# Issuing the experts' loop of a decoder trunk in a written order on every engine

## The chip, the cores and the metric

The kernel runs on one core of one Trainium2 chip. The metric is the device time of one execution in microseconds, lower is better. Before the change the median of three runs is 1376.91 us (1375.65 to 1377.59).

## The reference, cut to what matters

A trunk of two layers over 256 tokens of width 1024, float32 throughout. The change touches only the last block, the top-2-of-8 experts:

```python
logits = xt @ w_router                       # 256 x 8
top_logits, top_idx = lax.top_k(logits, 2);  gates = softmax(top_logits)
for e in range(8):                           # as blocks of gathered tokens
    y_e = (silu(x_e @ w_gate[e]) * (x_e @ w_up[e])) @ w_down[e]   # 1024 -> 3584 -> 1024
y[token] += gate * y_e[slot];  x = x + g2 * y;  out = rmsnorm(x) * final_gain
```

All eight experts are computed, so 8 x 3 x 1024 x 3584 float32 weights (336 MiB) are read once each.

## The kernel before

Layer 0, the pooling mixer and the router come first (to about 450 us). Then the experts' loop runs to the end.

**Blocks.** An expert's hidden width of 3584 is cut in seven blocks of 512 (`NJ`). A block is three weight tiles of 128 x 4096 float32: gate, up and down. The expert in place 0 has seven narrow blocks, done first. After that three wide places (1 to 3, up to 128 tokens) and four narrow places (4 to 7, up to 64 tokens) alternate in groups of seven blocks, in the order wide, narrow, wide, narrow, wide, narrow, narrow (`BLOCKS`, line 55). The down tile of a block is used two blocks after its gate and up tiles. Which expert stands at a place is found on the chip from the counts (`ordering`) and read into a register of SP before that expert's first load.

**Halves.** Each tile arrives as two halves of 128 x 2048 (1 MiB, `load`, line 126) in a ring of buffers: six of tag `raw`, four of `e8`, two that stay (`cb`, `T_l`), and `qk`, `a8`, `kd` for some loads at the start (`SPARE`, line 59). Each half is split into an upper and a lower part (`split`, line 112): ScalarE copies it rounded to `w_hi`, VectorE subtracts to `w_lo`. There are three pairs of `w_hi` and `w_lo` buffers (`N_SPL`), so a half can be split once TensorE has done with the half three before it. `raw` is free when `w_lo` is written.

**Matmuls.** A wide half takes 12 matmuls of 512 columns (`mm3`: hi times hi, hi times lo, lo times hi), a narrow one 8 (`mm2`: both parts of 64 tokens stand side by side in one 128-column stationary operand, and `fold_T` adds them with 16 small matmuls against `fold`).

**Around the matmuls.** `take_out` or `silu` empties a gate's or up's PSUM bank on ScalarE. `moe_T` (wide) or `fold_T` (narrow) turns the hidden block and splits it to `dT`. `prepare` gathers a place's tokens with 16 matmuls per half (`gather`, with its split in the same step). `combine` scales an expert's output by `g2_row` to `y_g`, splits it to `yp` and scatters it to `xs` with four `give` steps. Such steps wait in two lists and one is run after each tile.

**Order.** The program is traced in the order of the source, but the order in which each engine issues is chosen by a planner that takes what its own cost model thinks is ready first. `behind(...)` adds edges: the evacuation of a tile's PSUM bank and the turn of the previous block are queued behind the split of the last half of the next tile (`behind_next`, line 835).

Of the kernel before, what the change touches and what calls it, by code (L numbers as in the profile page):

```python
# [19 lines left out]
P = 128  # L20
# [44 lines left out]
def trunk(ctx, tc, x, cols, c_row, const, ada_0, ada, w_0, w_in, w_out, f_gu, f_dn, pool_w, m_g, m_u, m_d, out):  # L65
# [57 lines left out]

    ring = deque([("raw", N_RAW, ALWAYS)] * N_RAW)

# [10 lines left out]
    def weights(src, step=2048, held=((), (), (), ()), in_halves=False):  # L136

        parts, splits = [], []
        for h in range(0, src.shape[1], 2048):
            t = load(src[:, h:h + 2048], in_halves)  # L140
            hi = buf("w_hi", [2048], N_SPL, R)
            lo = buf("w_lo", [2048], N_SPL, R)
# [452 lines left out]
    n_blocks = NE * NJ  # L595
    expert = [0] + [None] * (NE - 1)

    def sources():

        def rows(a, i):  # L600
            p, j = BLOCKS[i]
            if p == 0:
                return a[j * P:(j + 1) * P, :]
            if expert[p] is None:
                expert[p] = nc.values_load(place_i[0:1, p - 1:p], engines=[SP], min_val=1, max_val=NE - 1,
                                           skip_runtime_bounds_check_because="a permutation of 1 to 7")
            return a[ds((expert[p] * NJ + j) * P, P), :]

        for i in range(n_blocks + 2):
            if i < n_blocks:  # L610
                yield rows(m_g, i)
                yield rows(m_u, i)
            if i > 1:
                yield rows(m_d, i - 2)

    srcs = sources()


    once = [ring[i][:2] + (1,) for i in range(2)]
# [32 lines left out]
    def ordering():  # L652
# [5 lines left out]
        cnt = small([NE], "cnt")  # L658
        nc.vector.tensor_copy(cnt, ps[:, 0:NE])
# [9 lines left out]
        nc.vector.tensor_reduce(rank, over.rearrange("p e i j -> p e (i j)"), axis=AX.X, op=ALU.add)  # L669
        at = tmp[:, 2 * N * N:3 * N * N].rearrange("p (r e) -> p r e", r=N)  # L670
# [11 lines left out]
        nc.vector.tensor_copy(place_i, place)  # L682
        placed = []
        for name, a in (("slot", slot), ("sel", sel), ("gate", gate)):
# [3 lines left out]
            placed.append(t)  # L688

# [11 lines left out]
        return place_i, placed, room, most_i  # L701
# [13 lines left out]
    def prepare(xe, slots, sels, narrow=False):  # L715


        oh = None
        ohT = buf("ohT", [T], N_OHT, R)
        ns = HALF if narrow else P  # L720

        def gather(n):
            nonlocal oh
            if n == 0:
                oh = one_hot(slots, sels, narrow)
            ps = tbank()[:, 0:4 * ns]
# [4 lines left out]
            ps = ps.rearrange("p (c t) -> p c t", c=4)  # L731
# [6 lines left out]
        def back():  # L738
            ps = tbank()
            for b in range(TB):  # L740
                nc.tensor.transpose(ps[:, tok(b)], oh[:, b], ident)
            nc.scalar.activation(ohT, ps[:, 0:T], AF.Copy)

        return xe, ohT, [lambda n=n: gather(n) for n in range(2)] + [back]
# [16 lines left out]
    def hidden(pg, pu):  # L761
        sg = w2([512], "sg")
        nc.scalar.activation(sg, pg, AF.Silu)
        hd = w2([512], "moe_h")
# [3 lines left out]
    def moe_T(hd):  # L768
        ps = transpose4(hd)
        th = buf("dT", [2, 4, P], 2, R, name="dT")  # L770
        split(th[:, 0], th[:, 1], ps.rearrange("p (c t) -> p c t", c=4))
        return th
# [6 lines left out]
    def fold_T(gu):  # L779
# [8 lines left out]
        nc.vector.tensor_mul(hd, ps[:, 1], sg)  # L788
        th = buf("dT", [4, 2, HALF], 2, R, name="dT")
        split(th[:, :, 0], th[:, :, 1], hd)  # L790
        return th
# [10 lines left out]
    def combine(ye, ohT, gates, g2_row, last=False):  # L802

        yp = buf("kd", [1 if last else 2, D], dt=F if last else R, name="yp")

        def take(n):
            c = slice(512 * n, 512 * (n + 1))
            t = yp[:, 0, c] if last else w2([512], "y_g")
            nc.vector.tensor_mul(t, ye[n], g2_row[:, c])
            if not last:  # L810
                split(yp[:, 0, c], yp[:, 1, c], t)

        def give(n, b):
            c = slice(512 * n, 512 * (n + 1))
            ps = tbank()
            if last:
                nc.tensor.matmul(ps, ohT[:, tok(b)].bitcast(F), yp[:, 0, c], start=True, stop=True)
            else:
                nc.tensor.matmul(ps, ohT[:, tok(b)], yp[:, 0, c], start=True, stop=False)
                nc.tensor.matmul(ps, ohT[:, tok(b)], yp[:, 1, c], start=False, stop=True)  # L820
            nc.vector.scalar_tensor_tensor(xs[:, b, c], ps, gates[b], xs[:, b, c], op0=ALU.mult, op1=ALU.add)

        return [lambda: (take(0), take(1))] + [lambda n=n, b=b: give(n, b) for n in range(2) for b in range(TB)]
# [8 lines left out]
    with behind(root, chosen):  # L832
        coming = weights(next(srcs), 1024)

    def behind_next():

        return behind(*coming.splits[len(coming.splits) // 2]) if coming else nullcontext()

    def advance():
        nonlocal coming  # L840
        at, src = coming, next(srcs, None)
        coming = None if src is None else weights(src)
        return at

    steps, first_steps = [], []

    def step():
        if first_steps or steps:
# [187 lines left out]
```

## Time and profile before

| what | value |
|---|---|
| median of 3 runs | 1376.91 us |
| the profiled execution | 1374.36 us, of which the span of its instructions is 1372.6 us |
| PE busy | 1316.0 us (96%) |
| DVE busy | 1217.4 us (89%) |
| ACT busy | 966.0 us (70%) |
| DMA | 477.30 MB, mean 348 GB/s |
| mean granted TensorE clock | 0.991 |

PE is TensorE, DVE is VectorE, ACT is ScalarE, SP issues all loads. Busy shares are averages over stages. Matmuls overlap each other in the pipeline, so a busy PE is not PE at its peak. Times below are from the start of the span. The experts' loop is cut into stretches at the start of a DVE split: 458.9 (half 2), 556.3 (half 38, the first of the alternating blocks), and then every 42 halves, that is every seven blocks, to 1340.8 (half 332 of 336).

### The profile page before, as it was taken

What the parts mean: (1) busy time and instruction counts of PE and PEld (TensorE: products, weight loads), DVE (VectorE), ACT (ScalarE), POOL (GpSimd) and SP (SyncE); (2) the same over time, 40 slices, a digit from 0 to 9 for tenths busy, and PEclk for the clock granted to TensorE, in tenths of its full rate; (3) what the DMA queues carried; (4) which work ended last, traced back from release to release, by engine and by line L of the source; (5) the groups of instructions that cost most, each with busy time, mean ns of one, the idle gap of its engine ahead of it and who ended that gap; (6) DMA issues with size and microseconds to landing.
All of it is one profiled execution on the core that took longest, in us unless ns stands there. A gap on an engine that the chain in (4) does not pass through costs nothing.

```text
span 1372.6 us, 16765 instructions
## 1 busy us (share of the span) xinstructions
PE 1316.0 (96%) x6146; PEld 1054.7 (77%) x6146; DVE 1217.4 (89%) x1119; ACT 966.0 (70%) x889; POOL 0.2 (0%) x4
## 2 busy tenths in 40 slices
PE   7999998999999999999999999999999999999996
PEld 5687877888887768778778877788778777777874
DVE  6889876998766799999989999989999989999997
ACT  6655465444435698878878877878877868788884
POOL 0000000000000000000000000000000000000000
PEclk9999999999999899999999999999999999999998
DMA  9976886899746999999999999999999999999960
GB/s 381 366 277 251 330 297 222 306 391 375 307 164 257 359 384 373 368 379 413 420 374 397 424 349 340 406 363 426 411 362 408 366 350 394 401 362 416 424 284 33
DMA packets 66474, 477.30 MB, mean 348 GB/s; under 512 B 7377, under 2 KB 7761, under 8 KB 8658
## 3 DMA queue, kind: packets, MB, share of 16 engines
q1 hardware_dynamic: 66386, 476.17, 88.6%
q8 instruction: 50, 0.82, 0.2%
q14 instruction: 38, 0.31, 0.1%
HBM read 475.10 MB, written 1.05 MB: 347 GB/s over the span
## 4 chain that ended last, share of the span: by engine, by line
PE 70%; DVE 15%; DMA 6%; ACT 4%; issue 4%; SPq 0%; DVEq 0%; ACTq 0%
PE bank L157 15%; PE bank L158 15%; PE bank L156 15%; DVE w_lo L113 11%; PE bank L749 8%; PE bank L748 7%; PE tbank L784 4%; DMA raw<-in_m_d_dram 3%; ACT w_hi L113 2%; DMA raw<-in_m_u_dram 2%; PE tbank L730 2%; PE tbank L256 1%; DVE raw L167 1%; DMA raw<-in_m_g_dram 1%; DMA col<-in_cols_dram 1%
## 5 line engine op out<-in xcount | busy, mean ns | idle before, releaser
L113 DVE TENSOR_TENSOR w_lo<-raw,w_hi 128x2048 fp32r<-128x2048 f32 (+1 forms) x413 | 907.8, 2225 | 91.2 <-ACT w_hi L113 87.3
L113 ACT ACTIVATE w_hi<-raw 128x2048 fp32r<-128x2048 f32 (+1 forms) x413 | 763.0, 1865 | 196.1 <-PE bank L158 147.4
L749 PE MATMUL bank<-w_lo,xe_n 128*128 128x512 f32 x560 | 230.9, 413 | 14.4 <-DVE w_lo L113 11.4
L748 PE MATMUL bank<-w_hi,xe_n 128*128 128x512 f32 x560 | 220.8, 395 | 0.0
L749 PEld LDWEIGHTS bank<-w_lo,xe_n 128*128 128x128 f32 x560 | 105.6, 189 | 59.9 <-DVE w_lo L113 40.5
L156 PE MATMUL bank<-w_hi,T_h 128*128 128x512 f32 x352 | 140.9, 401 | 3.1 <-ACT T_h L113 3.1
L157 PE MATMUL bank<-w_lo,T_h 128*128 128x512 f32 x352 | 139.2, 395 | 2.4 <-DVE w_lo L113 2.4
L158 PE MATMUL bank<-w_hi,T_l 128*128 128x512 f32 x352 | 139.2, 396 | 0.6 <-DVE T_l L113 0.5
L157 PE MATMUL bank<-w_lo,xe 128*128 128x512 f32 x336 | 132.8, 395 | 0.7 <-DVE w_lo L113 0.6
L156 PE MATMUL bank<-w_hi,xe 128*128 128x512 f32 x336 | 131.5, 391 | 0.0
L158 PE MATMUL bank<-w_hi,xe 128*128 128x512 f32 x336 | 131.0, 390 | 0.0
L748 PEld LDWEIGHTS bank<-w_hi,xe_n 128*128 128x128 f32 x560 | 105.8, 189 | 18.8 <-ACT w_hi L113 0.2
L167 DVE SCALAR_TENSOR_TENSOR raw<-raw,cb 128x1024 f32<-128x1024 f32 x96 | 114.4, 1218 | 0.0
L749 PE MATMUL bank<-w_lo,dT 128*128 128x512 f32 x280 | 104.5, 411 | 6.4 <-DVE w_lo L113 5.8
L157 PE MATMUL bank<-w_lo,dT 128*128 128x512 f32 x256 | 100.9, 394 | 0.9 <-DVE w_lo L113 0.8
L748 PE MATMUL bank<-w_hi,dT 128*128 128x512 f32 x280 | 99.8, 393 | 1.7 <-DVE dT L113 1.7
L158 PE MATMUL bank<-w_hi,dT 128*128 128x512 f32 x256 | 99.9, 390 | 0.0
L156 PE MATMUL bank<-w_hi,dT 128*128 128x512 f32 x256 | 93.5, 389 | 0.0
L156 PEld LDWEIGHTS bank<-w_hi,T_h 128*128 128x128 f32 x352 | 66.8, 190 | 17.6 <-ACT T_h L113 3.7
L157 PEld LDWEIGHTS bank<-w_lo,T_h 128*128 128x128 f32 x352 | 66.8, 190 | 16.6 <-DVE w_lo L113 2.8
L158 PEld LDWEIGHTS bank<-w_hi,T_l 128*128 128x128 f32 x352 | 66.9, 190 | 15.5 <-DVE T_l L113 1.5
L157 PEld LDWEIGHTS bank<-w_lo,xe 128*128 128x128 f32 x336 | 63.1, 188 | 17.1 <-DVE w_lo L113 4.7
(231 smaller groups left out, 1417.9 us busy)
## 6 DMA issues: line engine op xcount, KB each, us to landing
raw<-in_m_g_dram SPq DMA_DIRECT2D x112, 1024.0 KB, 7.1
raw<-in_m_u_dram SPq DMA_DIRECT2D x112, 1024.0 KB, 7.2
raw<-in_m_d_dram SPq DMA_DIRECT2D x112, 1024.0 KB, 7.2
raw<-in_ada_dram SPq DMA_DIRECT2D x48, 1024.0 KB, 7.1
raw<-in_f_gu_dram SPq DMA_DIRECT2D x22, 1024.0 KB, 6.5
raw<-in_w_in_dram SPq DMA_DIRECT2D x16, 1024.0 KB, 4.9
raw<-in_f_dn_dram SPq DMA_DIRECT2D x11, 1024.0 KB, 6.9
raw<-in_w_dram SPq DMA_DIRECT2D x8, 1024.0 KB, 7.7
```

What stands on the lines that cost most here:

```text
L113: return nc.scalar.activation(hi, src, AF.Copy), nc.vector.tensor_sub(lo, src, hi.bitcast(F))
L156: nc.tensor.matmul(ps, xh, wh, start=start, stop=False)
L157: nc.tensor.matmul(ps, xh, wl, start=False, stop=False)
L158: nc.tensor.matmul(ps, xl, wh, start=False, stop=stop)
L167: nc.vector.scalar_tensor_tensor(s, s, 1.0, cb, op0=ALU.mult, op1=ALU.mult, accum_out=mod[:, m:m + 1])
L256: nc.tensor.transpose(ps[:, i * P:(i + 1) * P], src[:, i * P:(i + 1) * P], ident)
L730: nc.tensor.matmul(ps[:, i * ns:(i + 1) * ns], xm[:, b, c], oh[:, b, 0:ns], start=(b == 0), stop=(b == TB - 1))
L748: nc.tensor.matmul(ps, x, wh, start=start, stop=False)
L749: nc.tensor.matmul(ps, x, wl, start=False, stop=stop)
L784: nc.tensor.matmul(ps[:, i, c], a[:, c * P:(c + 1) * P], fold, start=True, stop=True)
```

## The change

The loop is put in a region in which each engine issues in the order of the source (`tc.manual_schedule()`); the planner's choice and the `behind` edges are gone there. `PROGRAM` lists the 168 tiles: gate and up of block i, then down of block i-2. Each tile's turn emits, in this order: its matmuls; load and split of one half, four halves ahead; its evacuation; the turn of the previous block (the narrow one's split to `dT` one tile later); one step; load and split of a second half. A fourth pair of split buffers is made of `cb` and `T_l`, which leave the load ring, as does `qk` (now `y_g`). `gather` and its split, `back` and its copy, `give` and its add become steps of their own, and so do the parts of `ordering`; a step that leaves a PSUM bank full is followed by its partner. `f_row` and the load of the square-root table move to the end of the loop. Two matmuls of `ident` and `xs` ahead of the loop, whose result nothing reads, are dropped.

```diff
-SPARE = ((8, "a8", 2, 2), (11, "kd", 1, 3), (12, "qk", 1, 10), (12, "cb", 1, ALWAYS), (9, "T_l", 1, ALWAYS))
+SPARE = ((8, "a8", 2, 2), (11, "kd", 1, 3))
+PROGRAM = [("d", BLOCKS[i - 2]) if what == "d" else (what, BLOCKS[i]) for i in range(NE * NJ + 2) for what in "gud"
+           if (i > 1 if what == "d" else i < NE * NJ)]
+AHEAD = 4
+    halves = deque([("w_hi", "w_lo", N_SPL)] * N_SPL)
...
+    halves.append(("cb", "T_l", 1))
-    ps = tbank()
-    for _ in range(2):
-        nc.tensor.matmul(ps, ident, xs[:, 1, 0:512], start=True, stop=True)
+    def fetch(step=2048):
+        src = next(feed, None)
+        if src is not None:
+            t, (hi, lo) = load(src), halves_of()
+            for c in range(0, 2048, step):
+                split(hi[:, c:c + step], lo[:, c:c + step], t[:, c:c + step])
+            stream.append((hi, lo))
...
-        return xe, ohT, [lambda n=n: gather(n) for n in range(2)] + [back]
+        return xe, ohT, [hot, lambda: gather(0), lambda: parts(0), lambda: gather(1), lambda: parts(1) or back(), back_out]
...
-        return [lambda: (take(0), take(1))] + [lambda n=n, b=b: give(n, b) for n in range(2) for b in range(TB)]
+        def scaled():
+            to = y_g
...
+            for n in range(2):
+                nc.vector.tensor_mul(to[:, half(n)], ye[n], g2_row[:, half(n)])
+
+        def upper():
+            st["yp"] = buf("kd", [2, D], dt=R, name="yp")
+            for n in range(2):
+                nc.scalar.activation(st["yp"][:, 0, half(n)], y_g[:, half(n)], AF.Copy)
+
+        def lower():
+            yp = st["yp"]
+            for n in range(2):
+                nc.vector.tensor_sub(yp[:, 1, half(n)], y_g[:, half(n)], yp[:, 0, half(n)].bitcast(F))
...
+        steps = [scaled] if last else [scaled, upper, lower]
+        for n in range(2):
+            for b in range(TB):
+                steps += [lambda n=n, b=b: give(n, b), lambda n=n, b=b: add(n, b)]
+        return steps
...
+    def step():
+        nonlocal held
+        queue = held or first_steps or steps
+        if queue:
+            held = queue if queue.pop(0)() else None
...
+    with tc.manual_schedule():
+        while len(stream) < AHEAD:
+            fetch()
+        for n, (what, block) in enumerate(PROGRAM):
+            p, j = block
+            wide = WIDE[p]
+            if what == "d":
+                if j == 0:
+                    outs[p] = [bank(), bank()]
+                if block == BLOCKS[-1]:
+                    turn(block)
+                    while block not in ths:
+                        turn()
+                down(next_weights(), ths.pop(block), outs[p], j == 0, j == NJ - 1, not wide)
+                fetch()
+                if j == NJ - 1:
+                    while p == NE - 1 and (first_steps or steps):
+                        step()
+                    finish_combine(p)
+                    if p < NE - 1:
+                        steps.pop(-11)()
+            else:
+                if what == "g":
+                    while held or first_steps and first_steps[0] in ready[p][2]:
+                        step()
+                ps = up(next_weights(), ready[p][0], not wide)
+                fetch()
+                i = BLOCKS.index(block)
+                if what == "g":
+                    gates[block] = silu(ps) if wide else take_out(ps, "g_out")
+                    if i:
+                        turn(BLOCKS[i - 1])
+                else:
+                    sg = gates.pop(block)
+                    mid[block] = hidden(sg, ps) if wide else (sg, take_out(ps, "u_out"))
+                    turn()
+                    if block == (0, 0):
+                        gate, g2_row = gating()
+                        steps.extend([lambda it=ordering(known): next(it, None)] * 8)
...
+            step()
+            fetch()
+        f_row = row(y_gs[:, 1], col[:, C_FG:C_FG + KD])
+        table(AF.Sqrt, xs[:, 0, 0:1])
+        while steps:
+            step()
```

## Rows read from the trace of the kernel before

**Rows 1.** The view by windows: busy us (instructions) of PE, PEld, DVE, ACT, POOL; clock, DMA.

```profile
458.90:556.30 97.40, 92.50 (x482) 75.19 (x481) 90.92 (x91) 85.27 (x76) 0.00 (x0) 0.99 0.98 379
556.30:664.90 108.60, 106.59 (x488) 84.29 (x487) 104.99 (x66) 89.60 (x66) 0.00 (x0) 1.00 0.98 390
664.90:775.00 110.10, 108.91 (x519) 87.65 (x518) 101.72 (x62) 89.67 (x67) 0.00 (x0) 1.00 0.99 400
775.00:891.60 116.60, 112.49 (x530) 90.27 (x529) 112.28 (x79) 92.36 (x71) 0.00 (x0) 1.00 0.96 372
891.60:1006.50 114.90, 111.72 (x532) 89.41 (x531) 106.17 (x67) 91.20 (x70) 0.00 (x0) 1.00 0.98 394
1006.50:1124.60 118.10, 114.66 (x566) 93.45 (x565) 108.54 (x73) 92.41 (x73) 0.00 (x0) 1.00 0.97 376
1124.60:1235.80 111.20, 107.98 (x501) 85.77 (x501) 105.16 (x66) 89.61 (x68) 0.00 (x0) 1.00 0.98 384
1235.80:1340.80 105.00, 104.14 (x477) 82.94 (x476) 100.25 (x58) 88.87 (x64) 0.00 (x0) 1.00 0.88 366
```

**Rows 2.** Waits of DVE and of ACT, 556.3 to 1340.8: total, times, longest us.

```profile
DVE w_lo L113 <- ACT w_hi L113: 35.2, 55, 1.7
...
ACT w_hi L113 <- PE bank L158: 62.9, 79, 2.0
...
ACT xe_n L113 <- PE tbank L730: 12.4, 6, 3.8
```

**Rows 3.** The timeline of DVE and of ACT: splits back to back (start, us, count).

```profile
646.55 13.30 DVE L113 TENSOR_TENSOR w_lo<-raw,w_hi 128x2048 fp32r<-128x2048 f32 x6
...
1250.57 5.53 ACT L113 ACTIVATE w_hi<-raw 128x2048 fp32r<-128x2048 f32 x3 [0.32 <-ACT sg L763]
```

**Rows 4.** The chain of waits: start, us, what stood in it.

```profile
523.18 1.78 PE tbank L730 x16
...
531.09 1.73 PE tbank L784 x16
...
1187.47 0.50 PE bank L157
1187.97 0.23 PE bank L158
```

**Rows 5.** The timeline of the loop's start.

```profile
446.20 3.43 PE L627 MATMUL tbank<-xs,kp 128*128 128x512 f32 x4
...
458.90 2.28 DVE L113 TENSOR_TENSOR w_lo<-raw,w_hi 128x2048 fp32r<-128x2048 f32 x1
...
462.96 13.44 DVE L113 TENSOR_TENSOR w_lo<-raw,w_hi 128x2048 fp32r<-128x2048 f32 x6 [1.78 <-ACT w_hi L113]
```

**Rows 6.** The view by windows, five microseconds at the loop's start (columns as in Rows 1).

```profile
455.00:460.00 5.00, 5.00 (x21) 4.66 (x21) 1.86 (x3) 1.15 (x3) 0.00 (x0) 0.50 1.01 418
```

**Rows 7.** The timeline of the loop's end.

```profile
1338.59 4.49 DVE L113 TENSOR_TENSOR w_lo<-raw,w_hi 128x2048 fp32r<-128x2048 f32 x2
...
1343.80 1.31 ACT L113 ACTIVATE yp<-y_g 128x512 fp32r<-128x512 f32 x2 [0.85 <-DVE y_g L809]
...
1349.63 0.41 DVE L788 TENSOR_TENSOR h_n<-tbank,sg_n 128x256 f32<-128x256 f32 x1
...
1350.52 1.28 ACT L232 ACT_TABLE_LOAD   x1
1351.81 0.20 ACT L232 ACTIVATE tab<-xs 128x1 f32<-128x1 f32 x1
...
1352.63 0.50 PE L748 MATMUL bank<-w_hi,dT 128*128 128x512 f32 x1 [1.67 <-DVE dT L113]
...
1357.08 1.28 DVE L809 TENSOR_TENSOR yp<-bank,g_row 128x512 f32<-128x512 f32 x2
...
1359.05 1.54 DVE L821 SCALAR_TENSOR_TENSOR xs<-tbank,gate_p,xs 128x512 f32<-128x512 f32 x2 [0.69 <-PE tbank L817]
```

**Rows 8.** DMA issues by line: KB each, median us to landing.

```profile
raw<-in_m_g_dram SPq DMA_DIRECT2D x112, 1024.0 KB, 7.1
```

More of the change, by code (lines that the diff above doesn't have):

```diff
@@ L759, in up, with silu, hidden @@
         return ps
-    def hidden(pg, pu):
+    def silu(pg):
         sg = w2([512], "sg")
         nc.scalar.activation(sg, pg, AF.Silu)
+        return sg
+    def hidden(sg, pu):
         hd = w2([512], "moe_h")
@@ L800, in down, with combine @@
                     mm3(ye[n], th[:, 0, c], th[:, 1, c], wh, wl, first and c == 0, last and c == 3)
[L802 to L811, printed above, removed]
+    def combine(ye, ohT, gates, g2_row, y_g, last=False):
+        st = {}
+        half = lambda n: slice(512 * n, 512 * (n + 1))
+        def scaled():
+            to = y_g
+            if last:
+                st["yp"] = buf("kd", [1, D], name="yp")
+                to = st["yp"][:, 0]
+            for n in range(2):
[8 more added lines that the diff above has]
+                nc.vector.tensor_sub(yp[:, 1, half(n)], y_g[:, half(n)], yp[:, 0, half(n)].bitcast(F))
@@ L821, in give, with add @@
-            nc.vector.scalar_tensor_tensor(xs[:, b, c], ps, gates[b], xs[:, b, c], op0=ALU.mult, op1=ALU.add)
-        return [lambda: (take(0), take(1))] + [lambda n=n, b=b: give(n, b) for n in range(2) for b in range(TB)]
+                for i in range(2):
+                    nc.tensor.matmul(ps, ohT[:, tok(b)], yp[:, i, half(n)], start=(i == 0), stop=(i == 1))
+            return True
+        def add(n, b):
+            c = half(n)
+            nc.vector.scalar_tensor_tensor(xs[:, b, c], st.pop("ps"), gates[b], xs[:, b, c], op0=ALU.mult, op1=ALU.add)
@@ L832, in trunk @@
     with behind(root, chosen):
[L833 to L843, printed above, removed]
+        for _ in range(2):
+            fetch(1024)
     steps, first_steps = [], []
+    held = None
     def step():
-        if first_steps or steps:
-            (first_steps or steps).pop(0)()
@@ L851, in turned_of @@
[L851 to L852 removed]
+        nonlocal held
+        queue = held or first_steps or steps
+        if queue:
+            held = queue if queue.pop(0)() else None
     def picked(a, placed, p):
         return pick(a, 0) if p == 0 else pick(placed, p - 1)
[L857 to L868 removed]
+    y_gs = buf("qk", [2, D], name="y_g")
@@ L870, in prepare_next, with finish_combine @@
+    gates, mid, ths, outs, known = {}, {}, {}, {}, []
+    turning = None
+    def finish_combine(p):
+        steps.extend(combine(outs[p], ready[p][1], picked(gate, known[1][2], p), g2_row, y_gs[:, len(outs) % 2], p == NE - 1))
     def prepare_next(p):
+        slot_p, sel_p, _ = known[1]
         ready[p] = prepare(xe_of(p), pick(slot_p, p - 1), pick(sel_p, p - 1), not WIDE[p])
         first_steps.extend(ready[p][2])
[L876 to L904 removed]
@@ L905, in trunk, with turn @@
-    ths[n_blocks - 1] = turned_of(n_blocks - 1, mid)
-    down_of(n_blocks - 2)
-    while steps:
-        step()
-    last = coming
-    down_of(n_blocks - 1)
-    steps += combine(outs[NE - 1], ready[NE - 1][1], picked(gate, gate_p, NE - 1), g2_row, True)
-    with behind(last.splits[-1][0]):
-        table(AF.Sqrt, xs[:, 0, 0:1])
-    while steps:
-        step()
+    def turn(block=None):
+        nonlocal turning
+        if block is not None:
+            turning = block, (moe_T if WIDE[block[0]] else fold_T)(mid.pop(block))
+        if turning is not None:
+            th = next(turning[1])
+            if th is not None:
+                ths[turning[0]] = th
+                turning = None
@@ L917, in finish @@
+    place_i, _, room, most_i = known
     def finish():
@@ L947, in trunk @@
                 at = ds((e * NJ + j) * P, P)
-                hd = hidden(up(weights(m_g[at, :]), xe), up(weights(m_u[at, :]), xe))
-                down(weights(m_d[at, :]), moe_T(hd), ye, j == 0, j == NJ - 1)
-            for step in combine(ye, ohT, [ge[:, b] for b in range(TB)], g2_row):
+                hd = hidden(silu(up(weights(m_g[at, :]), xe)), up(weights(m_u[at, :]), xe))
+                down(weights(m_d[at, :]), next(moe_T(hd)), ye, j == 0, j == NJ - 1)
+            for step in combine(ye, ohT, [ge[:, b] for b in range(TB)], g2_row, y_gs[:, 0]):
                 step()
```

124 lines of the change are left out of this document (50 added, 74 removed).

## The prediction

> **What bounds the kernel now.** I read the view by windows first, cut where DVE begins a given split. In the seven stretches of seven blocks [rows 1] DVE is busy 739.1 of 784.5 us, and PE shows 99% in the fastest of them. So two engines are near full at once, and the idle 45.4 us of DVE in these seven, with 6.5 us in the stretch ahead of them, bound what a better order alone can win: 52 us. The waits say what the idle time is: DVE waits 35.2 us for the upper part of the next half, and ACT waits 62.9 us for TensorE to give back a split buffer [rows 2]. A half costs DVE 2.21 us back to back (13.30 for six, the last one 0.08 longer) and ACT 1.85 us (5.53 for three) [rows 3]. A matmul costs 0.23 us, the first one after a wait 0.50, 16 folds 1.73, 16 gathers 1.78 [rows 4]. Seven blocks are then 42 x 2.21 + 6.7 for turning the blocks (four narrow, two instructions of 0.41 each [rows 7]; three wide, two of twice that size) = 99.5 us of DVE, and 408 x 0.23 + 4 x 1.73 + 1.3 = 102 us of PE. The last stretch, which has neither a combine nor a gather, takes 105.0, with DVE idle for 4.75 of it [rows 1].
>
> What the steps add I fit to the same rows. The first stretch has one combine: 108.6 - 105.0 = 3.6 us. The second has one gather: 5.1 us. The sixth has a combine and `f_row`, so `f_row` is 2.6. All seven hold 6 combines and 5 gathers: 7 x 105.0 + 6 x 3.6 + 5 x 5.1 + 2.6 = 784.7, against 784.5 measured.
>
> **The change part by part. Start of the loop.** With three pairs the split of half 3 waits for TensorE's first half; DVE idles 1.78 us and starts it at 462.96 [rows 5]. With four it follows half 2, and half 4 starts near 463.0 instead of 465.2: -2 us.
>
> The two dropped matmuls are 3.43 us on PE ahead of the ranking matmuls [rows 5]; in their place PE mostly waits for DVE, so I count 0. The bounds are -1 and +2.5: in 455 to 460 the granted clock is 0.50, the lower level, though they ran 6 us earlier [rows 6], and another 5 us at that level would cost half of it. The Trainium skill ("TensorE: Matmul & The Clock Gate", What's actually happening) holds that the low clock is the default and activity releases it, which speaks against dropping them; by it the sum would be up to 2.5 us higher.
>
> **First stretch.** Past that 1.78 us, 4.7 us of DVE idle are left. I walked narrow blocks through the written order (each instruction at the later of its engine's turn and its input): DVE never waits, since ACT ends the later half's upper part 1.1 us before DVE wants it. One wait comes with `gating`, now one piece: Exp and its table load (1.28 us, as in rows 7) and two row copies sit ahead of the next upper part, about 3 us of idle DVE. So -1.7.
>
> **The seven stretches, without steps.** The fourth pair gives ACT one more half of lead, but the written order spends it. The split of a tile's second new half stands behind the evacuation and, after a narrow block, behind the folds (1.73 us after the gate's last matmul) and their Silu. Walking one group of 21 tiles: after the three fold turns ahead of a wide gate DVE idles 1.6, 0.8 and 0.8 us, at two wide downs 0.5 each, and 0.65 in small pieces: 4.85 of idle on 99.5 of work, 104.4 us per group against 105.0. That is -0.6 x 7 = -4. Bounds: -3 per group (two thirds of the idle gone) to +2.5 per group (half as much idle again).
>
> **Combines.** `scaled` (DVE) and `upper` (ACT) fall in the same tile, and the next upper part of a weight half is queued behind `upper`. DVE's next split waits for 1.31 of `upper` [rows 7] and 1.92 of the upper part: 3.2 us idle. Some of that replaces idle the group has anyway; the walk with a combine gives +5.6 against 3.6 measured, so +2.0 for places 0, 5, 2 and 6. For places 4 and 1 gather steps come in between, and the cost stays: together +8.
>
> **Gathers.** ACT's 12.4 us of waits for gather matmuls [rows 2] go, because the split comes one tile later. I take 3.0 us (PE 3.6 and DVE 1.5 per gather, each half hidden) for 5.1: -2.1 x 3. For wide places 2 and 3 the last gathered part stands behind a weight split on DVE, and PE waits some 2.3 us for it: +0.2 x 2. Together -6. `f_row` leaves this stage: -2.6.
>
> **End.** Place 3's combine comes with the third last tile, and nothing hides it. From the start of the split of half 332: splits and turn 2.2 + 0.35 + 2.2 + 2.2 = 6.95, `scaled` 1.28, `upper` 1.31, upper part 1.92, last split 2.28, `lower` 1.28, then the turn of the last block, which the order puts behind the down before it (0.41 + 0.42 + 0.42), and 16 matmuls, 3.95: 20.2 us. Now it is 1357.08 - 1340.8 = 16.3 [rows 7]: +3.9. After it, four adds of place 3 run, which were hidden (0.65 + 4 x 0.72 = 3.5), the second transposes and copy of `f_row` (0.45 + 0.65), the table load (1.28) and its one-column read of `xs` (0.20), which the next add must wait for: 6.2 us to the last expert's first add, against 1.97 now [rows 7]: +4.2. So +8.1, with bounds +4 and +10. The profile shows the table load at 1.28 us with the next activation 0.01 behind [rows 7]. The Trainium skill ("ScalarE: Activation LUTs", What ACT_TABLE_LOAD costs) adds a drain of about 1.38 us to each; by that the end would be 1.4 us later, and the trace does not agree.
>
> **Loads** cost nothing. A ring of ten halves covers 10 x 2.5 = 25 us against 7.1 from issue to landing [rows 8]. SP's order and register reads are the same.
>
> **Sum.** -2 - 1.7 - 4 + 8 - 6 - 2.6 + 8.1 = -0.2. The profiled execution took 1374.36 us (1.76 around the span), 2.55 under the median; the same difference on the median of 1376.91 gives 1376.7, so 1377.
>
> **The rivals.** *Given back in part only* (faster): the fourth pair absorbs the waits my walk leaves, so DVE's idle falls to 3 us per group (-12 for -4), and the combine's bubble falls where PE is the late one (+2 for +8). The sum is -14, about 1362. For it: ACT's 62.9 us of buffer waits is what one more pair attacks. Against: PE itself is 99% busy in the plain stretch.
>
> *Slower, by one mechanism*: ACT's lead of 1.1 us in front of the later half. Each of 56 blocks passes through evacuation and turn in order; a wait of 0.2 us per handoff is in my walk. If handoffs and interleaved steps eat more than those 1.1 us, each further 0.1 us stalls DVE in every block, 5.6 us. At 0.3 beyond, +17: 1394. For it: the planner could put a ready split ahead of a late evacuation, a fixed order can't. Against: PE and DVE alternate as the late one, which hides some.
>
> *The order is nearly what the planner had* (evacuations were already queued behind splits), and the end overlaps more than I think: 1376.
>
> **Chances.** Balance, as forecast (1370 to 1384 by itself): 0.44. Faster rival: 0.29. Slower rival: 0.20. Same order: 0.07. A measurement tells about 0.2%, 2.75 us, from no change. From balance 0.10 falls below that band, 0.19 in it and 0.15 above. So faster 0.39, same 0.26, slower 0.35. The range reaches into both rivals: 1355 to 1392.
>
> **What would show it.** After: DVE idle 30 to 45 us in the seven stretches; a gap of some 3 us on DVE behind the scaling of places 0, 5, 2 and 6, with ACT's split behind `yp`; no waits of ACT for gather matmuls; the last expert's first add 22 to 26 us after the split of half 332 begins, against 18 now. A loop with DVE idle under 25 us, or an end no longer than now, makes the prediction wrong on the fast side; ACT's splits regularly ending after DVE is free, on the slow side.

## The result, and the profile after

The changed kernel takes 1383.36 us (median of 5 runs, 1383.0 to 1390.71) against 1375.69 us before, run beside it (median of 5 runs, 1372.58 to 1377.59): ratio 1.0068, 95% interval 1.0039 to 1.0096. So it is slower by 0.7%, 5 to 13 us. The profiled execution has a span of 1381.0 us against 1372.6, a mean granted clock of 0.982 against 0.991.

The stretches after, cut at the same halves as [rows 1] (half 2, half 38, then every 42 halves; the last row is from half 332 to the end). The columns are those of [rows 1].

```profile
460.16:558.70 98.54, 89.51 (x448) 73.32 (x447) 91.45 (x89) 81.72 (x71) 0.00 (x0) 0.96 0.95 359
558.70:669.62 110.92, 107.95 (x511) 87.33 (x510) 104.78 (x67) 88.74 (x70) 0.00 (x0) 1.00 0.98 383
669.62:777.58 107.96, 106.52 (x519) 88.16 (x518) 100.95 (x61) 88.20 (x68) 0.00 (x0) 1.00 1.00 411
777.58:892.67 115.09, 109.74 (x533) 90.86 (x532) 109.34 (x74) 91.93 (x72) 0.00 (x0) 1.00 0.98 386
892.67:1004.70 112.03, 109.65 (x525) 90.18 (x524) 105.29 (x68) 90.09 (x70) 0.00 (x0) 0.98 0.99 403
1004.70:1120.93 116.23, 109.75 (x550) 91.61 (x549) 107.69 (x72) 89.22 (x68) 0.00 (x0) 1.00 0.98 377
1120.93:1234.96 114.03, 108.06 (x505) 87.97 (x504) 107.08 (x68) 90.17 (x69) 0.00 (x0) 1.00 0.98 382
1234.96:1340.03 105.07, 104.22 (x493) 85.61 (x491) 100.48 (x58) 88.69 (x67) 0.00 (x0) 1.00 0.93 384
1340.03:1381.00 40.97, 23.41 (x89) 16.24 (x87) 22.68 (x30) 12.78 (x21) 0.00 (x0) 0.80 0.08 28
```

The seven stretches take 781.3 us (784.5 before): some are shorter (second, third, fourth, fifth), those of places 0 and 6 are longer (first, sixth), and the plain one is what it was. The loop's start up to half 38 ends 2.4 us later (558.70 against 556.3), and the end is 9.2 us longer (41.0 against 1372.6 - 1340.8 = 31.8). 2.4 - 3.2 + 9.2 = +8.4, the difference of the spans.

What stands in the waits of the seven stretches (558.7 to 1340; total us, times, longest us), against [rows 2]:

```profile
DVE w_lo L118 <- ACT w_hi L118: 42.8, 52, 2.5
...
ACT w_hi L118 <- PE bank L168: 55.4, 63, 2.4
ACT sg_n L820 <- PE tbank L818: 27.6, 25, 1.1
ACT w_hi L118 <- PE bank L778: 20.7, 17, 3.2
ACT yp L853 <- DVE y_g L848: 16.4, 4, 5.3
...
ACT xe_n L118 <- PE tbank L753: 1.7, 2, 0.9
...
PE tbank L867 <- DVE xs L872: 10.7, 7, 2.9
```

The waits for gather matmuls went (12.4 to 1.7), as the change meant. But ScalarE now waits 16.4 us in four pieces for `y_g` (7.1 us in six before), and VectorE's waits for the upper part grew from 35.2 to 42.8. The last line is new: TensorE's scatter matmuls (`give`) wait 10.7 us for VectorE's add to `xs`, which empties a PSUM bank and stands behind a weight split on VectorE's queue. Before, no wait of TensorE for that add is among its waits in these stretches. Neither kernel is held up by its loads here: in the seven stretches ScalarE waits 8.1 us for loads before, and neither it nor VectorE waits for one after. The timeline of place 0's combine shows the first two at once:

```profile
597.62 1.28 DVE L848 TENSOR_TENSOR y_g<-bank,g_row 128x512 f32<-128x512 f32 x2
601.40 4.49 DVE L118 TENSOR_TENSOR w_lo<-raw,w_hi 128x2048 fp32r<-128x2048 f32 x2 [2.50 <-ACT w_hi L118]
...
598.33 1.23 ACT L853 ACTIVATE yp<-y_g 128x512 fp32r<-128x512 f32 x2 [5.28 <-DVE y_g L848]
599.47 3.71 ACT L118 ACTIVATE w_hi<-raw 128x2048 fp32r<-128x2048 f32 x2
```

ScalarE had nothing to wait for but `y_g`: it stood 5.28 us with `yp` at the head of its queue, ran it, and only then began the next half's upper part, for which VectorE then stood 2.50 us. The same 2.50 us stands behind the scaling at 992.8, 1093.2, 1192.8 and 1347.0 (places 5, 2, 6 and 3), and behind those of places 4 and 1 it doesn't.

The end, from the same timeline (compare [rows 7]):

```profile
1346.97 1.28 DVE L848 TENSOR_TENSOR y_g<-bank,g_row 128x512 f32<-128x512 f32 x2
1350.75 2.29 DVE L118 TENSOR_TENSOR w_lo<-raw,w_hi 128x2048 fp32r<-128x2048 f32 x1 [2.50 <-ACT w_hi L118]
...
1355.54 0.80 PE L778 MATMUL bank<-w_hi,dT 128*128 128x512 f32 x1 [6.37 <-DVE dT L118]
1356.13 0.63 PE L779 MATMUL bank<-w_lo,dT 128*128 128x512 f32 x1
...
1365.79 1.25 ACT L203 ACTIVATE y_g<-tbank 128x512 f32<-128x512 f32 x2 [10.76 <-PE tbank L197]
1367.06 1.28 ACT L242 ACT_TABLE_LOAD   x1
1368.36 0.20 ACT L242 ACTIVATE tab<-xs 128x1 f32<-128x1 f32 x1
1368.59 1.41 DVE L872 SCALAR_TENSOR_TENSOR xs<-tbank,gate_p,xs 128x512 f32<-128x512 f32 x2 [1.69 <-ACT tab L242]
```

The last expert's first add comes 28.6 us after the split of half 332 begins (1368.59 - 1340.03; 18.3 before). The copies of `f_row`, the table load and its one-column read stand one behind the other ahead of it.

### The profile page after: what moved, and what is told of

Its sections match the earlier page's. It is cut to its first block, busy times and chain, and to the rows that moved or that the text cites. A ratio compares the mean times of both kernels' runs of the same rounds, so it can differ in the third digit from the quotient of the medians.

```text
span 1381.0 us, 16731 instructions
## 1 busy us (share of the span) xinstructions
PE 1307.7 (95%) x6142; PEld 1067.0 (77%) x6142; DVE 1214.6 (88%) x1119; ACT 957.5 (69%) x888; POOL 0.2 (0%) x4
## 4 chain that ended last, share of the span: by engine, by line
PE 42%; DVE 13%; issue 7%; ACT 3%; DVEq 0%; ACTq 0%
DVE w_lo L118 10%; PE bank L779 8%; PE bank L778 8%; PE bank L166 7%; PE bank L167 7%; PE bank L168 6%; PE tbank L818 3%; ACT w_hi L118 2%; PE tbank L753 2%; PE tbank L867 1%; DVE xs L872 1%; DVE dT L118 1%; DVE yp L858 1%; DVE y_g L848 0%; DVE moe_h L798 0%
## 5 line engine op out<-in xcount | busy, mean ns | idle before, releaser
L779 PE MATMUL bank<-w_lo,xe_n 128*128 128x512 f32 x560 | 223.6, 399 | 6.7 <-DVE w_lo L118 5.7
L778 PE MATMUL bank<-w_hi,xe_n 128*128 128x512 f32 x560 | 224.5, 401 | 0.3 <-ACT w_hi L118 0.3
L779 PE MATMUL bank<-w_lo,dT 128*128 128x512 f32 x280 | 112.3, 401 | 8.2 <-DVE w_lo L118 8.2
L778 PE MATMUL bank<-w_hi,dT 128*128 128x512 f32 x280 | 111.6, 398 | 6.4 <-DVE dT L118 6.4
L166 PE MATMUL bank<-w_hi,dT 128*128 128x512 f32 x256 | 100.0, 391 | 0.0
L167 PE MATMUL bank<-w_lo,dT 128*128 128x512 f32 x256 | 99.7, 390 | 0.0
L168 PE MATMUL bank<-w_hi,dT 128*128 128x512 f32 x256 | 99.7, 390 | 0.0
```

The costliest lines, as they stand in the source:

```text
L166: nc.tensor.matmul(ps, xh, wh, start=start, stop=False)
L167: nc.tensor.matmul(ps, xh, wl, start=False, stop=False)
L168: nc.tensor.matmul(ps, xl, wh, start=False, stop=stop)
L778: nc.tensor.matmul(ps, x, wh, start=start, stop=False)
L779: nc.tensor.matmul(ps, x, wl, start=False, stop=stop)
```

## The experiments

The ratio of each run is to the kernel before on the same chip; the changed kernel was not run again beside them, so runs are compared with it by these ratios and by their profiles. The stretches are from each run's profile, in us:

```
               half 2   first  the seven stretches                        end   span
before          458.9    97.4  108.6 110.1 116.6 114.9 118.1 111.2 105.0  31.8  1372.6
after           460.2    98.5  110.9 108.0 115.1 112.0 116.2 114.0 105.1  41.0  1381.0
upper_later     459.3    98.7  109.0 108.0 113.5 108.2 112.8 110.9 105.0  35.7  1361.1
tail_order      460.2    98.6  110.9 108.0 115.1 112.1 116.3 114.0 110.9  36.3  1382.3
gating_early    456.2    97.6  110.9 108.0 118.3 112.0 117.2 114.0 105.1  40.4  1379.7
matmuls_back    457.7    98.6  110.9 108.0 115.1 112.1 117.0 114.9 105.8  40.0  1379.9
fill_last       457.3    98.7  111.0 108.0 118.3 112.0 118.0 114.9 105.7  39.8  1383.6
three_pairs     459.4   104.0  115.7 114.6 121.3 118.2 123.6 116.4 110.5  40.7  1424.4
before_4pairs   442.1   112.1  107.7 109.2 116.6 114.9 117.9 110.4 104.2  31.5  1366.6
best1           457.5    96.3  109.0 108.0 115.1 108.2 112.8 110.9 106.0  33.0  1356.8
best2           454.4    96.0  109.0 108.0 113.7 111.9 114.2 110.5 105.9  33.0  1356.6
best3           457.6    94.5  109.7 106.7 110.4 111.6 112.7 112.5 106.3  33.6  1355.6
```

In before_4pairs the planner puts the split of half 2 ahead of the first tile's, so its first two columns can't be compared with the others; its half 38 begins at 554.2.

Theory: the loss is in a few places where the written order puts an instruction on an engine's queue in the very tile that makes its input: at the combines, at the gating and at the end. Rival: the order as such is late everywhere, or the fourth pair took something from the loads (the waits above already speak against the loads).

**upper_later.**

```diff
-        steps = [scaled] if last else [scaled, upper, lower]
+        steps = [scaled] if last else [scaled, lambda: None, upper, lower]
...
-                        steps.pop(-11)()
+                        steps.pop(-12)()
```

> The changed kernel with `upper` of a combine one tile after `scaled` (an empty step between them). Theory (ScalarE queues the two copies of `yp` and then the weight half behind the scaling, VectorE stands 2.5 us per combine): the 2.50 us gap of VectorE ahead of its split at 601.40 goes, and the like at places 5, 2 and 6 and in the last tiles; 4 x 2 us in the seven stretches and 2 to 4 us in the last one, so 10 us off the changed kernel's 1383. Rival (the gap replaces idle time that VectorE has anyway, TensorE being nearly full): the stretches keep their lengths within 1 us, and only the last one, where nothing else is late, gives 2 to 4 us.

1362.91 us (1361.5 to 1364.01), ratio 0.992 (0.9905 to 0.9934): one empty step turns 0.7% slower into 0.8% faster. The timeline at the same place:

```profile
596.89 1.28 DVE L848 TENSOR_TENSOR y_g<-bank,g_row 128x512 f32<-128x512 f32 x2
598.09 4.48 DVE L118 TENSOR_TENSOR w_lo<-raw,w_hi 128x2048 fp32r<-128x2048 f32 x2
...
600.18 1.15 ACT L853 ACTIVATE yp<-y_g 128x512 fp32r<-128x512 f32 x2
```

VectorE goes on without a gap. Compared half by half, the split behind each of the five scalings comes 2.58 to 2.59 us earlier, together 12.9 of the 19.9 us of span, and the stretches with one such gap are 1.9, 3.8, 3.4 and 3.2 us shorter. At place 0 a quarter of the gap had stood in place of other idle time; at the others the stretch gains the whole gap and 0.6 to 1.2 us more. So the rival falls. Of the other 7.0 us, 0.7 lie ahead of half 38, 2.0 in these four stretches, 1.6 in the third stretch, which has no gap of this kind, and 2.7 at the end, where the last down starts after a wait of 2.57 us, not 6.37, and runs 5.5 us, not 6.7. I did not take these apart further.

**tail_order.**

```diff
...
+                if block == BLOCKS[46]:
+                    while held:
+                        step()
+                    f_row = row(y_gs[:, 1], col[:, C_FG:C_FG + KD])
+                if block == BLOCKS[-2]:
+                    turn(BLOCKS[-1])
+                    while BLOCKS[-1] not in ths:
+                        turn()
+                    table(AF.Sqrt, one)
+                down(next_weights(), ths.pop(block), outs[p], j == 0, j == NJ - 1, not wide,
+                     (0, 2, 4, 2) if block == BLOCKS[-1] else (0, 0, 0, 0))     # steps ahead of each chunk
...
```

> The changed kernel with four things moved at its end: the turn of the last block ahead of the down before it, `f_row` ahead to the down of the tenth last block, the load of the square-root table (its one column read from a constant, not from `xs`) ahead of the second last down too, and place 3's four scatter steps between the chunks of the last down. Theory (the end is a chain in which each of these stands alone): the time from the split of half 332 to the end falls from 41.0 to about 32 to 34 us, and the last down no longer starts at the lower clock because TensorE waits less in front of it; 7 to 9 us off. Rival (the end is bounded by the splits of the last halves and by the last down, with those steps beside them): 2 us or less.

1388.32 us, ratio 1.0109 (1.0092 to 1.0126): no gain. The end did get 4.7 us shorter (36.3), between the 7 to 9 of the theory and the 2 of the rival. The gap of 2.50 us at place 3 is still in it, and the last down still starts at the lower clock, behind a wait of TensorE of 5.07 us (granted 0.50 in 1360 to 1365). And the plain stretch, in which `f_row` now stands, got 5.8 us longer:

```profile
1238.43 0.82 PE L197 MATMUL tbank<-kp,col 128*128 128x128 f32 x4 [3.11 <-DVE xs L874]
...
1245.46 2.29 DVE L118 TENSOR_TENSOR w_lo<-raw,w_hi 128x2048 fp32r<-128x2048 f32 x1 [4.89 <-ACT w_hi L118]
...
1243.51 1.92 ACT L118 ACTIVATE w_hi<-raw 128x2048 fp32r<-128x2048 f32 x1 [3.63 <-PE bank L168]
```

The second transposes of `f_row` wait 3.11 us on TensorE for a bank that VectorE's add has to free; the down's matmuls are queued behind them, ScalarE waits for these, and VectorE for ScalarE: 4.89 us. It is the mechanism of the combine once more, made by the experiment itself. TensorE's clock falls behind the same wait (granted 0.88 in 1235 to 1240, 0.78 in the next 5 us), so its price is in the 5.8 us too. Under the planner `f_row` cost 2.6 by the prediction's fit.

**gating_early.**

```diff
+        gate = gating()                       # mx, sub
         while len(stream) < AHEAD:
             fetch()
+        nc.scalar.activation(gate, gate, AF.Exp)
...
-                        gate, g2_row = gating()
+                        g2_row = buf("g_row", [D], name="g2_row")
+                        steps.extend(g2_steps(g2_row))   # transposes, copy, one tile apart; then the rest of the gates
```

> The changed kernel with the gates' two small VectorE instructions and their exponential put ahead of the first gate tile, where ScalarE waits 2.60 us for TensorE, and the two copies of `g2_row` made steps of one tile each. Theory (the gating as one piece stops ScalarE, and VectorE idles 1.98 + 1.17 + 0.33 + 0.53 us behind it): the first stretch falls from 98.5 to about 95.5 us, 3 us off. Rival (those gaps stand behind the loads or behind TensorE's low clock near 474): 98 us, no change.

1380.82 us (1377.2 to 1385.86), ratio 1.0052 (1.0032 to 1.0073). From the split of half 4 to that of half 38 it takes 90.0 us (463.81 to 553.82) against 93.9 after (464.76 to 558.70): 3.9 us off, as the gaps of the gating were 1.98 + 1.17 + 0.33 + 0.53 = 4.0. (From half 2 it shows less, since that split begins earlier here, between the gathers.) The four other runs that keep the gating and the fourth pair take 94.0 to 94.3 us for the same halves. TensorE's low clock at that place went away with the gating. It isn't what cost the time: upper_later and fill_last have about twice as much of it there (0.57 and 0.74 in 470 to 480 in upper_later) and are 0.3 us longer, not 4. The first three lines are of the changed kernel, the last is of this run:

```profile
475.69 2.29 DVE L118 TENSOR_TENSOR w_lo<-raw,w_hi 128x2048 fp32r<-128x2048 f32 x1 [1.98 <-ACT w_hi L118]
479.15 2.29 DVE L118 TENSOR_TENSOR w_lo<-raw,w_hi 128x2048 fp32r<-128x2048 f32 x1 [1.17 <-ACT w_hi L118]
...
470.00:475.00 5.00, 1.57 (x7) 1.39 (x8) 3.29 (x8) 3.71 (x6) 0.00 (x0) 0.90 1.00 375
...
470.00:475.00 5.00, 5.00 (x33) 4.49 (x33) 4.90 (x7) 4.98 (x6) 0.00 (x0) 1.00 0.99 352
```

The exponential costs nothing ahead of the loop:

```profile
455.86 1.28 ACT L949 ACT_TABLE_LOAD   x1
457.16 0.22 ACT L949 ACTIVATE gate<-gate 128x16 f32<-128x16 f32 x1
```

Yet the third stretch, whose code is the same, took 118.3 and not 115.1. TensorE waits 1.97 us there at 798.7, where the second gather stands until VectorE has split the first one's rows, and 2.95 us at 834.6, where a scatter matmul stands until VectorE's add to `xs` gives back a PSUM bank (1.98 and 2.94 after). This time its clock fell behind both. The windows of this run:

```profile
800.00:805.00 5.00, 4.32 (x20) 4.19 (x21) 5.00 (x5) 1.20 (x1) 0.00 (x0) 0.66 0.96 356
835.00:840.00 5.00, 2.47 (x8) 1.97 (x9) 5.00 (x4) 2.07 (x2) 0.00 (x0) 0.85 1.00 365
840.00:845.00 5.00, 5.00 (x20) 4.00 (x19) 4.55 (x3) 3.35 (x3) 0.00 (x0) 0.81 1.01 365
```

and of the changed kernel (the same work is some 3 to 5 us later):

```profile
800.00:805.00 5.00, 3.57 (x18) 2.75 (x16) 5.00 (x5) 3.92 (x5) 0.00 (x0) 1.00 1.02 419
805.00:810.00 5.00, 4.45 (x28) 4.00 (x29) 5.00 (x4) 1.80 (x2) 0.00 (x0) 1.00 0.99 367
835.00:840.00 5.00, 2.84 (x15) 2.16 (x13) 5.00 (x5) 4.76 (x5) 0.00 (x0) 1.00 0.92 293
840.00:845.00 5.00, 4.21 (x18) 3.48 (x19) 5.00 (x5) 2.14 (x2) 0.00 (x0) 1.00 0.96 356
...
1000.00:1005.00 5.00, 5.00 (x16) 3.46 (x16) 5.00 (x6) 5.00 (x5) 0.00 (x0) 0.69 0.91 315
```

A granted 0.66 over 5 us has lost 5 x 0.34 = 1.7 us of TensorE's work at the full clock; 0.85 and 0.81 together make the same (5 x 0.15 + 5 x 0.19). Two falls are 3.4 us, and 118.3 - 115.1 = 3.2. fill_last has the third stretch at 118.3 with the same two falls, and the runs without them (after, tail_order, matmuls_back) have 115.1. The changed kernel had its one at 1000 to 1005, behind a wait of 1.82 us; there it didn't lengthen the fourth stretch (112.0 in gating_early too, which has none there). So a fall's price in time depends on the place.

**matmuls_back.** The two matmuls that the diff drops are put back.

> The changed kernel with the two dropped matmuls of `ident` and `xs` put back ahead of the loop. Theory (without them TensorE is at the lower clock from 445 to beyond 460, and half 4 has to wait for its first half): the clock in 445 to 455 is back near 0.7 to 0.8, the split of half 2 starts near 459 and that of half 4 near 463 and not 464.8; 1.3 to 2 us off. Rival (the start is set by VectorE, the clock there is beside it): no change, within 0.5 us, or 1 us slower since they take 3.43 us of TensorE.

1386.69 us (1381.7 to 1389.12), ratio 1.0099 (1.0082 to 1.0116): no gain, and the clock did not come back (0.50 from 445 to 460). The split of half 2 does begin 2.5 us earlier (457.7), but that was won ahead of the two matmuls: `sel` is ready at 446.2 and not 449.1, as it is in fill_last (446.3), which hasn't got them. From `sel` to the first gather it is 3.63 us here, as before, and 3.15 to 3.16 in the six runs without them, so here they cost 0.47 us. That isn't so everywhere: with them it is 3.18 in before_4pairs, where they start 3.7 us ahead of `sel`, and 4.25 in best3.

Whether they bring the clock back this one run can't tell, but the gathers in the traces of the other runs say more (32 matmuls; first to last line: before, after, this run, best1):

```profile
452.16 5.95 PE L730 MATMUL tbank<-oh,xm 128*128 128x64 f32 x32 [1.75 <-DVE oh L708]
...
452.27 7.09 PE L753 MATMUL tbank<-oh,xm 128*128 128x64 f32 x32 [1.66 <-DVE oh L730]
...
449.81 7.06 PE L757 MATMUL tbank<-oh,xm 128*128 128x64 f32 x32 [1.75 <-DVE oh L734]
...
453.55 6.14 PE L772 MATMUL tbank<-oh,xm 128*128 128x64 f32 x32 [1.75 <-DVE oh L749]
```

None of the six traces without the two matmuls has a moment of full clock in 450 to 455 (granted 0.50, gathers 7.09 us each). Of the six with them three have (before 0.84, best1 0.84, best2 0.64; gathers 5.95, 6.14 and 6.14 us) and three have not (here, before_4pairs, best3; 7.06 to 7.09). So they may help, by 1.1 us at most in the gathers, and with one trace of each kernel this stays open.

The prediction weighed a rule of the Trainium skill here ("TensorE: Matmul & The Clock Gate", What's actually happening): the low clock is the default, and activity releases it. The six traces without the matmuls agree with it, and three of the six with them do not show the release; so the rows lean its way and don't decide it.

**best1.** upper_later, gating_early, matmuls_back and tail_order together, with `f_row` as steps:

```diff
+                if block == BLOCKS[46]:
+                    f_row = y_gs[:, 1]
+                    steps.extend(row_steps(f_row, col[:, C_FG:C_FG + KD], lambda: None))
```

> The changed kernel with `upper` one tile later, the early gates, the two matmuls put back, and the end as in tail_order, but with `f_row` as three steps (transposes in one tile, copy in the next) queued behind place 6's combine and not as one piece ahead of a down. Theory (each of these removes a wait in which one engine's queue stands for another, and they add): from 1363 with the later `upper` alone, 2.5 us off at the start, 3 to 5 in the first stretch, 4 to 5 at the end, and `f_row` costs under 1 us in the last stretch (it cost 5.8 us in one piece): 1350 to 1354. Rival (the parts hide each other): 1358 to 1363, with the 5.8 us of `f_row` still there.

1359.24 us (1356.49 to 1360.4), ratio 0.9877 (0.9857 to 0.9896): faster than both kernels, by 1.2% and by some 1.9%. `f_row` in steps costs 0.9 us in the plain stretch (106.0), the end is 33.0, the start to half 38 is 4.9 us shorter than after. The sum was 5 to 9 us too good: the end's gains overlap (5.3 and 4.7 alone, 7.9 together), the 2.5 us expected of the matmuls had no ground in matmuls_back, and the third stretch has a fall of the clock (granted 0.73 in 800 to 805; 115.1 us against 113.5 in upper_later).

**three_pairs** and **before_4pairs** take the fourth pair out of the changed kernel and put it, alone, into the kernel before.

```diff
-    halves.append(("cb", "T_l", 1))       # three_pairs, with AHEAD = 3
...
+    halves.append(("cb", "T_l", 1))       # before_4pairs, with cb and T_l out of SPARE
```

> The changed kernel without the fourth pair of split buffers: three pairs, three halves ahead, the loads in the same ring of ten. Theory (the pair is what pays for the fixed order: with three, a half's upper part waits for TensorE's current tile in every tile): the plain last stretch goes from 105.1 to 115 us or more, the whole to 1440 or more. Rival (the order alone gives the time, the fourth pair is cover that is used up behind the evacuations): plain stretch 105 to 107, whole within 1383 to 1395.

> The kernel before with the fourth pair alone (`cb` and `T_l` out of the load ring, as split buffers), the order still the planner's. Theory (ScalarE's 62.9 us of waits for a split buffer in the seven stretches shrink, and VectorE's 35.2 us of waits for the upper part with them): plain stretch under 104 us, 5 to 15 us off the kernel before. Rival (TensorE and VectorE are near full in turn, and the edges that tie evacuations to splits keep the order): within 3 us of the kernel before.

three_pairs: 1426.49 us, ratio 1.037 (1.0353 to 1.0388). before_4pairs: 1370.47 us, ratio 0.9963 (0.9949 to 0.9977). The plain stretch of the one and of the other:

```profile
1273.15:1383.67 110.52, 106.00 (x482) 83.12 (x481) 100.34 (x58) 88.57 (x64) 0.00 (x0) 1.00 0.90 359
```

```profile
1230.97:1335.18 104.21, 102.87 (x477) 83.22 (x477) 99.33 (x58) 86.71 (x65) 0.00 (x0) 1.00 0.93 389
```

Both theories named the right side. That of three_pairs had the size too large (1440 or more), that of before_4pairs (5 to 15 us) is met at its lower edge. In the written order the pair is worth some 42 us (1426 against 1383, or the two ratios), under the planner some 5. So the change without its fourth pair costs about 51 us (1426.49 against 1375.63), and the pair pays most of it back. That the pair is the room for splits which stand behind evacuations and turns is an argument, though the waits fit it: with three pairs VectorE waits 66.3 us for upper parts in the seven stretches, with four 42.8.

before_4pairs also shows that waits are not time. The planner's kernel with the fourth pair waits 24.9 us for TensorE's split buffers where it waited 62.9, and 24.5 us for upper parts where it waited 35.2, and its seven stretches are only 3.5 us shorter (781.0 against 784.5).

**fill_last.**

```diff
                     turn(block)
+                    ps = tbank()
+                    for _ in range(3):
+                        nc.tensor.matmul(ps, ident, xm[:, 1, 0:512], start=True, stop=True)
```

> The changed kernel with three matmuls whose result nothing reads (of `ident` and `xm`, 512 columns) behind the last block's folds, where TensorE waits 6.37 us for VectorE. Theory (TensorE's clock is at its lower level in the last down because it idled ahead of it): the last down's 16 matmuls take 0.23 us each from the first, 3.7 us and not 6.6, and the end gets 2 to 2.5 us shorter. Rival (the lower clock there comes from something else, or the filler delays the down): no gain, or up to 1 us longer.

1385.61 us, ratio 1.0071 (1.0055 to 1.0088). The filler took 2.79 us and left 3.75 of the gap, and the last down still met the lower clock, for a shorter time:

```profile
1352.79 2.79 PE L943 MATMUL tbank<-xm,kp 128*128 128x512 f32 x6
1359.34 0.50 PE L778 MATMUL bank<-w_hi,dT 128*128 128x512 f32 x1 [3.75 <-DVE dT L118]
...
1363.03 0.45 PE L779 MATMUL bank<-w_lo,dT 128*128 128x512 f32 x1
```

Its 16 matmuls took 5.5 us, not 6.7, and the end is 1.1 us shorter, half of what was expected. A filler that covers the whole gap wasn't tried, and the total can't tell 1.1 us.

**best2** puts more room between steps (the one-hot rows a tile earlier, an empty step ahead of the first scatter), **best3** adds two more pairs and reads six halves ahead from a ring of six.

```diff
-        steps = [scaled] if last else [scaled, lambda: None, upper, lower]
+        steps = [scaled] if last else [scaled, lambda: None, upper, lower, lambda: None]
...
+        ready[p][2][0]()
+        ready[p][2][0] = lambda: None
...
-    halves.append(("cb", "T_l", 1))
+    halves.extend([("cb", "T_l", 1)] + [("e8", "e8", N_E8)] * 2)     # best3, AHEAD = 6
```

> best1 with more room between steps that hand over from VectorE to TensorE: a place's one-hot rows are built when its gather is announced, one tile ahead of the first gather, and one empty step stands between `lower` and the first scatter matmul. Theory (TensorE's gaps of 1.3 to 2.3 us at these handoffs, five in best1, can drop its clock: the one at 796.7 did, 1.6 us in the third stretch): no gap above 1.5 us in the seven stretches, third stretch 113.5, and less spread between executions; 1 to 4 us off best1's 1359. Rival (behind such a gap TensorE catches up, since the weights are ready): same as best1 within 1 us.

> best2 with six pairs of split buffers (the four `e8` buffers leave the load ring and make two pairs), splits six halves ahead, and a load ring of six. Theory (the pairs are what the fixed order needs: the fourth gave 43 us, VectorE still idles about 35 us in the seven stretches, 30 of them behind the upper part): plain stretch 103, seven stretches from 770 to 745 to 755 us. Rival (loads: in the second stretch DMA already moves 411 GB/s, 433 at most in any 5 us, 101.6 us for a stretch's 44.04 MB, and with six buffers each VectorE stall stops it too): no gain, or 5 to 20 us slower, with waits for `raw` by the DMA in ScalarE's list.

best2: 1361.79 us, ratio 0.9918 (0.9898 to 0.9938); best3: 1359.4, ratio 0.9898 (0.9877 to 0.9918). Neither beats best1. In best2 gaps of 1.45 to 2.33 us on TensorE are still there in the seven stretches, two of five at other places than in best1. best3 has the shortest third stretch (110.4), but the plain one is 106.3 and VectorE still waits 30.9 us for upper parts. Its rival had no gain and waits for loads in ScalarE's list, and both came: 11.9 us in all, where best1 has none. Whether these waits are what ate the gain isn't shown; two more pairs, taken out of the load ring, gained nothing here.

What holds best1 to 770 us in the seven stretches isn't shown by an experiment. In its second stretch PE is busy 106.5 of 108.0 us, and DMA has a busy share of 1.00. Over all seven the longest wait of TensorE is the one that the fixed order brought, of a scatter matmul for VectorE's add:

```profile
PE tbank L888 <- DVE xs L893: 8.4, 7, 2.3
```

Four of best1's five gaps on TensorE over 1.3 us end with that add, and three of best2's five, whose empty step stands ahead of the first scatter and not ahead of the bank's return; in best3 the waits for it are 13.9 us. A spare bank or an earlier add was not tried.

## Why the prediction was right or wrong

It said 1377 us, no change by balance, and a range of 1355 to 1392. The time is 1383.36, in the range and 0.5% above the forecast: by its own bound of 0.2% the changed kernel is slower, which had 0.35. In the span the sum was -0.2, and +8.4 was measured. That it isn't further off is in part luck: a term that was 3 us too dear hid part of two that were 4 and 6 us too cheap. By its steps:

- **Start and first stretch (-2 - 1.7 forecast, +2.4 measured): the step that failed most.** The fourth pair did give its 1.7 us between half 2 and half 4 (4.60 us against 6.27). But the loop's start was counted at 0 (bounds -1 and +2.5), and half 2 began 1.3 us later, so that half 4 came 0.4 us earlier, not 2: `sel` 0.6 us, and 0.7 us between it and half 2, where the gathers ran at the lower clock (1.1 us) and the dropped matmuls gave back 0.47. In the first stretch 3 us of idle VectorE were forecast, all at the gating; 7.1 us stand there (98.54 - 91.45), somewhat more than before (6.5). The gating's part is 4.0, and "VectorE never waits" elsewhere was wrong: 0.80 us stand ahead of half 5 and 0.99 at 543.5.
- **The seven stretches without steps (-4 forecast, +0.3 measured).** The plain stretch is 105.07 against 105.03. The walk's idle time was right (4.85 us forecast, 105.07 - 100.48 = 4.59 measured). Its work was not: the 99.5 us put together from single instructions stand against 100.25 us of busy VectorE in [rows 1], and against 100.48 after. Measured idle against walked idle, 4.75 and 4.85, would have said no gain.
- **Combines (+8 forecast).** Place and cause were right: 2.50 us at places 0, 5, 2 and 6. The walk took 3.2 us of gap (the upper part started earlier, behind the first half of `y_g`) and then let 1.2 us of it hide. In fact the four stretches with a gap are 12.3 us shorter without it (upper_later), where 8 were forecast. The first stretch's combine is 110.9 - 105.1 = 5.8 us, where 5.6 was forecast.
- **Gathers (-6).** The second stretch's gather is 108.0 - 105.1 = 2.9 us, where 3.0 was forecast. TensorE's waits for VectorE's add to `xs` (10.7 us) have no term in the forecast.
- The seven together: -4.6 forecast, -3.2 measured. That is near by luck: without steps they are 4.3 us worse than forecast, and the steps in them (combines, gathers, `f_row`) take 45.8 us and not 49.1.
- **End (+8.1 forecast, +9.2 measured).** The parts were all there. What I hadn't counted is TensorE's clock: it idles 6.37 us ahead of the last down and runs it at the lower level, 6.7 us for 3.95. The shorter gap at place 3 gave some of that back. The last expert's first add comes 28.6 us after half 332 and not 22 to 26, and what stands behind it is 1.1 us shorter than before, which brings the sum near again.

Of the signs named beforehand, the gap behind the scaling and the end of the waits for gathers came (2.50 us; 1.7 us left of 12.4). VectorE's idle time in the seven stretches is 45.7 us, at the upper edge of 30 to 45 and the same as before (45.4), and the first add is outside.

Of the rivals, *given back in part only* had its place right in that the gaps can be taken away at little price, but the change as made doesn't do it. *Slower by the handoffs' lead* did not happen with four pairs; with three (three_pairs) the plain stretch is 5.4 us longer, which fits it. The condition I named for the slow side, ScalarE's splits regularly late, is not what made it slower: of the 42.8 us of VectorE's waits for upper parts 10.0 are the four gaps at the combines, and the other 32.8 are less than the 35.2 before. Against the kernel before, the time was lost at the start and at the end, and the gaps at the combines used up most of what the seven stretches had to gain (767.4 us in upper_later, 781.3 here, 784.5 before).

## What to carry to other kernels

In a fixed order, an instruction must not stand in the tile that makes its input if the engine's next work feeds another bound engine: put it one tile later. One empty step was worth 20 us here, more than a fourth pair of buffers was under the planner. Helpers that go back and forth between engines (a gating, a row built by transposes and copies) have to be cut into steps first. What the engine's queue holds back counts too: an add that empties a PSUM bank, put behind a long split, makes the next matmul into that bank wait. And a gap on TensorE is priced with its clock: compare several executions before a difference of 2 or 3 us between two stretches with equal code is put down to an edit.

## What was not expected of the hardware

Gaps of 1.45 to 3.1 us on TensorE, inside a loop in which the changed kernel has it busy over 94% in each of the seven stretches, were followed by the lower clock in some executions and not in others. Each of these falls took 1.7 us of TensorE's work. In time it was 1.6 us a fall in the third stretch (gating_early, fill_last), 0.8 in the fifth at 1103 (matmuls_back, behind a wait of 1.89 us: granted 0.83 in 1100 to 1110, and 117.0 us against 116.2), and none can be seen in the fourth stretch of the changed kernel, at whose end its fall lies. The shortest such gap was 1.45 us, at 1227 in matmuls_back: granted 0.96 in 1225 to 1230 and 0.70 in the next 5 us; in the changed kernel the clock stayed up behind the same gap. The five executions of the changed kernel show it in the whole: granted clock 0.981 to 0.982 at 1383.0 to 1384.55 us, and 0.976 at 1390.71. DMA moved 411 GB/s over the whole second stretch, and in best1 at most 434 in any 5 us.
